# A hybrid decoder step on one core: the sample's state step moved out of the scan, and eight more gate blocks computed as Strassen pairs

## The chip, the core and the metric

The kernel runs on one core of a Trainium2 chip. The core has a matrix engine (TensorE, "PE" in the profile; its weight loads are listed apart as "PEld"), a vector engine (VectorE, "DVE"), an engine for activations and copies (ScalarE, "ACT"), a general engine (GpSimd, "POOL") and a queue engine that issues most of the DMAs (SyncE, "SP"); ACT issues some DMAs too, on a queue of its own. The metric is the device time of one execution in microseconds. The kernel before takes 2536.3 us, the median of 3 runs (2535.32 to 2539.43).

## What is computed

One layer of a decoder for a prompt of 1024 tokens and a sample group of 8 sequences with one token each. Both share all weights, so the kernel carries their 1024 + 8 = 1032 columns through every product together. What matters here, cut from the reference:

```python
splits = [int(v) for v in np.cumsum(IN_SIZES)[:-1]]
sc_b, sc_c, sc_x, z, xbc, dt_raw, q, gates = jnp.split(xn @ w_in, splits, axis=-1)
...
xbc_c, ssm_conv_new = causal_depthwise_conv(xbc, ssm_hist, ssm_conv_w)
xbc_c = jax.nn.silu(xbc_c + ssm_conv_b)
xs, bm, cm = jnp.split(xbc_c, [SSM_D_INNER, SSM_D_INNER + SSM_GROUPS * SSM_STATE], axis=-1)
...
y_ssd, ssm_new = ssd_fn(xs, dt, a, bm, cm, ssm_s0)
...
g_a, g_b, g_c = jnp.split(jax.nn.sigmoid(gates), N_BRANCHES, axis=-1)
merged = g_a * y_a + g_b * y_b + g_c * y_c
```

For the prompt, `ssd_fn` is a chunked scan (8 chunks of 128 tokens, 32 heads in 4 groups). For the sample it is one step of the recurrence, on a state of 32 heads x 64 x 128 for each of the 8 sequences:

```python
s = s * jnp.exp(dtt * a)[..., None, None] + (dtt[..., None] * xt)[..., None] * bh[:, :, None, :]
return s, jnp.einsum('bhpn,bhn->bhp', s, ch)
```

All products are float32, split into a high and a low part, so that each product of weights and activations is three matmuls (high x high, high x low, low x high).

## The kernel before

Everything is laid out with features on the 128 partitions and the 1032 columns in the free dimension. `w_in` is worked through in blocks of 128 output features. There are two ways to compute blocks.

- **Plain block** (`gemm`, line 180): 8 slices of the contraction x 3 split products x 3 column parts of 344 = 72 matmuls.
- **Strassen pair** (`strassen`, line 279): two blocks at once, as seven products of 4 x 3 x 2 = 24 matmuls of 258 columns, 168 in all. It also needs sums of weights (`V.tensor_add` in lines 305 and 306, `st_adds2`), splits of these sums (`st_split`: the high part on ACT, line 224, the low part on DVE, line 225), copies of the products out of PSUM (ACT, lines 296, 315, 318) and combinations of them (DVE, lines 320, 331, 333). The seven products run through three PSUM tiles; some of them are overwritten while the pair is still under way, so that PE can go on only when a copy or a combination has read them.

Work that is to run beside the matmuls is cut into pieces (functions in the deque `pend`). `tick()` takes one piece. A plain block calls it `pace[0]` times, spread over its 8 contraction slices; a pair calls it three times (lines 311, 327, 334). The pieces set an order of priority: a list scheduler orders each engine's instructions at build time, by this order and by its own estimates of when operands are ready. Each engine is given its list in that order.

The order of work around the change:

1. Six pairs of z blocks, with the memory keys and values as pieces (lines 1206 to 1208).
2. The pair stage (lines 1213 to 1230). First the xbc pair (17, 21), then for each of four groups: an xbc pair, three pairs for the short convolution (`sc_pairs`, two "C" pairs and a "B" pair), another xbc pair and one gate pair (`gate_pair`, line 764). After that a z pair, and the xbc pairs (18, 22) and (19, 23); in the last one the activations' second half is restored (`plain`, line 1226). An xbc pair also runs the depthwise convolution of both blocks on DVE (`xbc_conv`, line 707).
3. The scan (lines 1236 to 1306). Four groups of pieces run beside plain blocks: 8 q blocks, 16 gate blocks (8 to 23), then the 8 blocks of the first output projection (`out_part`). A group has 40 pieces: loading its activations, the scan's 8 chunks in three pieces each (`first`, `second`, `third`), then the gating with z and the group norm. With `pace[0] = 5` the 160 pieces take 32 plain blocks.
4. Attention and the remaining 16 projection blocks, then the last projection, the merge, and the feed-forward part.

The sample's state step lies in the scan's pieces: `s_load` (line 927: the state of one sequence and group, 256 KB, and the broadcast B and C rows, 128 KB, both by SP), `s_step` (line 934: 4 activations that decay the state, 4 that form the update, one addition of 512 columns on DVE) and `s_read` (line 943: the store of the new state, 256 KB, a product of 512 columns and a reduction on DVE). There are 32 such steps, 8 in each group. `bc_rows` (line 777) prepares the B and C rows of a group: two PE transposes, a copy and a store. Some of these pieces are held back behind named instructions with `tc.issue_after`.

Of the kernel before, what the change touches and what calls it, by code (L numbers as in the profile page):

```python
# [41 lines left out]
def tile_kernel(ctx: ExitStack, tc, a, o):  # L42
# [135 lines left out]
    pace = [3]  # L178

    def gemm(w, acts, name, width=P, off=0):  # L180

        hi, lo = w
        ps = mm_ps(name)
        nk = len(acts)
        marks = {nk * i // pace[0] for i in range(pace[0])}
        for k, (ah, al) in enumerate(acts):
            if k in marks:
                tick()
            ks = slice(k * width + off, k * width + off + P)
            for i, (wt, x) in enumerate(((hi, ah), (hi, al), (lo, ah))):  # L190
                for n in range(NCH):
                    PE.matmul(  # L192
                        ps[:, n, :CW], wt[:, ks], x[:, n * CW : (n + 1) * CW],
                        start=(k == 0 and i == 0), stop=(k == nk - 1 and i == 2),
                    )
        return ps
# [332 lines left out]
    dpar = cn.tile([P, 16], F32, tag="dpar", name="dpar")  # L529

# [212 lines left out]
    def plain_pair(col, dst, i, nm, func, hook=None):  # L743
# [7 lines left out]
        pa = strassen(  # L751
            wblock(w_in, col + i * P), wblock(w_in, col + (i + 1) * P), xforms, f"{nm}{i}", pa_["s"], outs,
            hook=hook,
        )
# [9 lines left out]
    def gate_pair(i):  # L764
        plain_pair(C_G, gt_d, i, "G", AF.Sigmoid)
# [11 lines left out]
    def bc_rows(g, bcg):  # L777

        ps = sm_ps(f"psbc{g}")
        PE.transpose(ps[:NS, :P], bcg[0][:, T:TT], ident)  # L780
        PE.transpose(ps[:NS, P : 2 * P], bcg[1][:, T:TT], ident)
        t = ev_tile(f"bcr{g}", (NS, 2, P))
        S.copy(t, b3(ps[:NS, : 2 * P], 2))
        SY.dma_start(bc_d[g], t)

    def ssd_pieces(g, xg, bcg):
# [8 lines left out]
        def load(c):  # L795
            nm = f"{g}_{c}"
            r = sp_tile([P, HPG, P], "r", "r" + nm, 3)
            live[c] = r
            return SY.dma_start(r, ac_d[g, c].unsqueeze(0).to_broadcast([P, HPG, P])).ins
# [16 lines left out]
        def first(c):  # L816
# [16 lines left out]
            state["xdt"] = V.tensor_tensor(  # L833
                b3(xdt, HPG), b3(xp, HPG), bc(dtT[:, c, hs].unsqueeze(2), [P, HPG, 64]), op=ALU.mult
            ).ins
# [50 lines left out]
        def decay(c):  # L886

            s_new = sp_tile([P, 512], "s", f"s{g}_{c}")
            ins = G.tensor_tensor(  # L889
                b3(s_new, HPG), b3(state["s"], HPG), bc(cdec[:, c, hs].unsqueeze(2), [P, HPG, 64]),  # L890
                op=ALU.mult,
            )
            state["next"] = s_new
            return ins.ins
# [11 lines left out]
        def s_skip():  # L906
            for t in range(4):
                V.scalar_tensor_tensor(
                    xg[t][:, T:TT], xg[t][:, T:TT], dpar[:, g * 4 + t : g * 4 + t + 1], hold["ys"][:, t, :],
                    op0=ALU.mult, op1=ALU.add,  # L910
                )

        hold = {}

        def s_prep():
            xd = sp_tile([P, 4, NS], "xds", f"xds{g}", 1)
            for t in range(4):
                V.tensor_mul(xd[:, t, :], xg[t][:, T:TT], dts[:, g * 4 + t, :])
            hold["xd"] = xd
            hold["ys"] = sp_tile([P, 4, NS], "ys", f"ys{g}", 1)  # L920

        def s_rows(t, b):
            return t[0, b, hs].rearrange("h p n -> (h p) n").rearrange("(t q) n -> q t n", q=P)

        samp = {}

        def s_load(b):
            st = sp_tile([P, 4, P], "st", f"st{g}_{b}", 3)
            SY.dma_start(st, s_rows(a["state_ssm"], b))
            bcb = sp_tile([P, 2, P], "bcb", f"bcb{g}_{b}")  # L930
            SY.dma_start(bcb, bc_d[g, b].unsqueeze(0).to_broadcast([P, 2, P]))
            samp[b] = (st, bcb)

        def s_step(b):
            st, bcb = samp[b]
            for t in range(4):
                S.activation(st[:, t], st[:, t], AF.Copy, scale=es[:, g * 4 + t, b : b + 1])  # L937
            xb = sp_tile([P, 4, P], "xb", f"xb{g}_{b}", 1)
            for t in range(4):
                S.activation(xb[:, t], bcb[:, 0], AF.Copy, scale=hold["xd"][:, t, b : b + 1])  # L940
            V.tensor_add(st, st, xb)  # L941

        def s_read(b):
            st, bcb = samp.pop(b)
            SY.dma_start(s_rows(o["s_ssm"], b), st)
            xb = ev_tile(f"xc{g}_{b}", (P, 4, P))
            V.tensor_tensor(xb, bc(bcb[:, 1:2, :], [P, 4, P]), st, op=ALU.mult)
            V.tensor_reduce(hold["ys"][:, :, b : b + 1], xb, axis=AX.X, op=ALU.add)

        def head():  # L950
            load(0)
            load(1)
            s_prep()
            prep(0)
            s_load(0)
            s_load(1)
# [3 lines left out]
        for c in range(NCK + 1):  # L960
            def p1(c=c):
                if c < NCK:
                    first(c)
                if c + 2 < NCK:
                    state["load"] = load(c + 2)
                if c > 1:
                    with tc.issue_after(state["xdt"] if c < NCK else state["sum"]):
                        with tc.issue_after(state["load"]):
                            s_read(c - 2)

            def p2(c=c):
                if c > 0:
                    state["sum"] = third(c - 1)
                    with tc.issue_after(state["sum"]):
                        if c < NCK:
                            with tc.issue_after(decay(c)):
                                s_step(c - 1)
                        else:
                            s_step(c - 1)
                if c + 1 < NCK:  # L980
                    with tc.issue_after(state["bT"]):
                        prep(c + 1)
                    if c + 1 > 1:
                        s_load(c + 1)

            def p3(c=c):
                if c < NCK:
                    second(c)
                else:
                    final()  # L990
                    s_read(NCK - 1)
# [232 lines left out]
    xbc_pair(18, 22)  # L1224
# [5 lines left out]
    xbc_pair(19, 23, plain)  # L1230
# [9 lines left out]
    for i in range(8, 24):  # L1240
# [41 lines left out]
    for g in range(GROUPS):  # L1282
# [13 lines left out]
        pend.extend([load_group, None, lambda g=g, bcg=bcg: bc_rows(g, bcg)])  # L1296
# [4 lines left out]
    pace[0] = 5  # L1301
# [562 lines left out]
```

## Time and profile before

| | |
|---|---|
| median of 3 runs | 2536.3 us |
| profiled execution | 2535.69 us |
| its span, first to last instruction | 2533.2 us |
| mean granted TensorE clock | 0.994 |
| PE busy | 2475.3 us (98%) |
| DVE busy | 1502.6 us (59%) |
| ACT busy | 1070.8 us (42%) |
| DMA, mean over the span | 156 GB/s |

A page of the profile describes one execution. It gives the busy time of each engine, the chain of waits that ended last (followed back from the last instruction, each step to what released it), the costliest groups of instructions by source line, and the DMA queues. The trace behind it answers for a window of time, a line or a tile. A row of the windows view lists, after the two ends of the window, its length and then for PE, PEld, DVE, ACT and POOL the busy time with the number of instructions in brackets, then the granted clock, the share of the DMA engines that is busy and GB/s. A row of the chain has its start, its length, the engine and tile, the line, and the number of instructions merged. Ends of matmuls are modelled, and a few per cent of the matmul records are missing, so lengths in the chain are the safer measure for PE.

### The profile page before, as it was taken

The numbers are of one execution on the slowest core, as the hardware profiler recorded it, in microseconds if no ns is written. First come the engines' busy times: TensorE is split into PE (matmuls) and PEld (weight loads), VectorE is DVE, ScalarE is ACT, GpSimd is POOL, SyncE is SP. The second block draws the span as 40 slices with busy tenths as digits, with TensorE's granted clock in tenths as the row PEclk, the third lists the DMA queues.
The fourth block names the chain that finished last, engine by engine and source line by source line (L and its number), as shares of the span: only waits on it lengthen the run. The fifth ranks groups of instructions, "written<-read, shape, count | busy, mean of one in ns | idle before, by whom it ended". The sixth has DMA issues, their size and how long they took to land.

```text
span 2533.2 us, 44306 instructions
## 1 busy us (share of the span) xinstructions
PE 2475.3 (98%) x18505; PEld 2408.9 (95%) x18505; DVE 1502.6 (59%) x2262; ACT 1070.8 (42%) x1783; POOL 115.1 (5%) x139
## 2 busy tenths in 40 slices
PE   7999999999999999999999989999999999999998
PEld 5999999999999999999989888999999999999998
DVE  6754575666666675757687662444776444463326
ACT  6544434343524665867554341223443333341202
POOL 0100000000000121212020000000000000000000
PEclk9999999999999999999999999999999999999999
DMA  6344422322323777676778977944442222274211
GB/s 203 101 155 151 126 84 85 92 87 83 99 76 126 226 226 232 202 240 213 263 232 288 313 254 239 303 144 151 145 135 92 84 68 86 74 240 136 75 34 68
DMA packets 351590, 394.68 MB, mean 156 GB/s; under 512 B 15814, under 2 KB 289302, under 8 KB 351383
## 3 DMA queue, kind: packets, MB, share of 16 engines
q1 hardware_dynamic: 332238, 338.90, 42.9%
q10 hardware_dynamic: 19153, 52.96, 5.5%
q8 instruction: 145, 2.38, 0.4%
q14 instruction: 54, 0.44, 0.1%
HBM read 283.57 MB, written 108.45 MB: 155 GB/s over the span
## 4 chain that ended last, share of the span: by engine, by line
PE 86%; DVE 6%; DMA 5%; ACT 2%; issue 1%; SPq 0%; DVEq 0%; ACTq 0%
PE po L192 12%; PE pd L192 8%; PE ps_g L192 6%; PE pm L1622 4%; PE ps_q L192 4%; PE py L858 1%; PE pss L876 1%; PE po L850 1%; PE ps_z L192 1%; PE X17m L237 1%; PE G2m L237 1%; PE B6m L237 1%; PE X12m L237 1%; PE C5m L237 1%; PE X6m L237 1%
## 5 line engine op out<-in xcount | busy, mean ns | idle before, releaser
L1764 DVE TENSOR_TENSOR x<-pd,x 128x1032 f32<-128x1032 f32 x24 | 29.5, 1230 | 127.2 <-PE pd L192 127.2
L805 ACT ACTIVATE r<-r,acum 128x128 f32<-128x128 f32 x256 | 78.6, 391 | 5.3 <-DMA r<-ac_d 4.8
L1263 DVE TENSOR_TENSOR gt<-po,gt 128x1032 f32<-128x1032 f32 x24 | 29.5, 1230 | 56.5 <-PE po L192 56.5
L837 POOL TENSOR_TENSOR xdd<-xdt,decst 128x512 f32<-128x512 f32 x32 | 48.6, 1518 | 311.3 <-DVE xdt L833 311.3
L940 ACT ACTIVATE xb<-bcb,xds 128x128 f32<-128x128 f32 x128 | 41.9, 391 | 45.7 <-DMA bcb<-bc_d 44.2
L644 DVE SCALAR_TENSOR_TENSOR ax<-u,prm,ax 128x1024 f32<-128x1024 f32 x44 | 56.3, 1280 | 0.2 <-ACT ax L641 0.2
L937 ACT ACTIVATE st<-st,es 128x128 f32<-128x128 f32 x128 | 42.4, 391 | 19.0 <-DMA st<-in_state_ssm_dram 11.3
L831 DVE TENSOR_TENSOR r<-r,cbm 128x1024 f32<-128x1024 f32 x32 | 39.1, 1221 | 12.5 <-ACT r L806 11.2
L867 DVE SCALAR_TENSOR_TENSOR x<-x,dpar,yt 128x128 f32<-128x128 f32 x128 | 36.4, 347 | 14.4 <-ACT yt L865 13.6
L858 PE MATMUL py<-r,xdt 128*64 128x128 f32 x512 | 35.0, 279 | 1.5 <-issue 1.5
L889 POOL TENSOR_TENSOR s<-s,cdec 128x512 f32<-128x512 f32 x28 | 35.4, 1265 | 20.9 <-DVE s L882 20.2
L876 PE MATMUL pss<-xdd,bT 128*128 128x512 f32 x64 | 33.3, 601 | 2.0 <-ACT bT L830 1.8
L806 ACT ACTIVATE r<-r 128x1024 f32<-128x1024 f32 x32 | 33.8, 1056 | 0.3
L1551 DVE TENSOR_TENSOR gt<-po,gt 128x1032 f32<-128x1032 f32 x8 | 9.9, 1232 | 39.3 <-PE po L192 39.3
L858 PEld LDWEIGHTS py<-r,xdt 128*64 128x64 f32 x512 | 27.3, 136 | 5.8 <-issue 2.4
L854 DVE TENSOR_TENSOR yt<-po,ea 128x512 f32<-128x512 f32 x28 | 19.3, 688 | 22.2 <-PE po L850 22.2
L1629 DVE TENSOR_TENSOR x<-pm,xT 128x516 f32<-128x516 f32 x16 | 11.1, 695 | 35.7 <-PE pm L1622 35.6
L850 PE MATMUL po<-bc,s 128*128 128x128 f32 x224 | 29.9, 276 | 2.1 <-DVE s L882 2.1
L850 PEld LDWEIGHTS po<-bc,s 128*128 128x128 f32 x224 | 28.2, 191 | 3.3 <-DVE s L882 3.0
L1372 DVE SCALAR_TENSOR_TENSOR kc<-kc,qb 128x256 f32<-128x256 f32 x64 | 23.8, 418 | 12.3 <-DMA qb<-qs_d 8.6
L941 DVE TENSOR_TENSOR st<-st,xb 128x512 f32<-128x512 f32 x32 | 29.6, 926 | 0.0
L1384 ACT ACTIVATE pr<-psa,mx 128x256 f32<-128x256 f32 x32 | 14.8, 471 | 32.0 <-DVE mx L1382 31.2
(8793 smaller groups left out, 8815.8 us busy)
## 6 DMA issues: line engine op xcount, KB each, us to landing
gt<-gt_d SPq DMA_DIRECT2D x32, 516.0 KB
r<-ac_d SPq DMA_DIRECT2D x32, 512.0 KB
mg_d<-gt SPq DMA_DIRECT2D x24, 516.0 KB
mg<-mg_d SPq DMA_DIRECT2D x24, 516.0 KB
xs_d<-ax ACTq DMA_DIRECT2D x22, 516.0 KB
hr<-h_d SPq DMA_DIRECT2D x22, 516.0 KB
x<-xs_d SPq DMA_DIRECT2D x16, 516.0 KB
zs<-zs_d SPq DMA_DIRECT2D x16, 516.0 KB
```

The costliest lines, as they stand in the source:

```text
L192: PE.matmul(ps[:, n, :CW], wt[:, ks], x[:, n * CW : (n + 1) * CW], start=(k == 0 and i == 0), stop=(k == nk - 1 and i == 2),)
L237: PE.matmul(ps[:, n, :HC], wt[:, ks], x[:, n * HC : (n + 1) * HC], start=(start and kt == 0 and i == 0), stop=(kt == 3 and i == 2), skip_g ...
L644: V.scalar_tensor_tensor(acc[:, :T], u[:, j : j + T], w[j], acc[:, :T], op0=ALU.mult, op1=ALU.add)
L805: S.activation(r[:, j, :], r[:, j, :], AF.Relu, scale=-1.0, bias=acum[:, c, h : h + 1])
L831: V.tensor_tensor(r, r, bc(cbm.unsqueeze(1), [P, HPG, P]), op=ALU.mult)
L837: G.tensor_tensor(b3(xdd, HPG), b3(xdt, HPG), bc(decst[:, c, hs].unsqueeze(2), [P, HPG, 64]), op=ALU.mult)
L850: PE.matmul(po[:, t * P : (t + 1) * P], state["s"][:, t * P : (t + 1) * P], bcg[1][:, cs], start=True, stop=True,)
L858: PE.matmul(py[hp : hp + 64, (h // 2) * P : (h // 2 + 1) * P], xdt[:, h * 64 : (h + 1) * 64], r[:, (h % 2) * 4 + h // 2, :], start=True, s ...
L876: PE.matmul(pss, bT, xdd, start=True, stop=True)
L937: S.activation(st[:, t], st[:, t], AF.Copy, scale=es[:, g * 4 + t, b : b + 1])
L940: S.activation(xb[:, t], bcb[:, 0], AF.Copy, scale=hold["xd"][:, t, b : b + 1])
L1622: PE.matmul(ps[:, n, :HC], wt[:, ks], x[:, half * HT + n * HC : half * HT + (n + 1) * HC], start=(k == 0 and i == 0), stop=(k == KD - 1 an ...
```

## The change

- The sample's 32 state steps leave the scan's pieces. After both xbc pairs of a group, 13 pieces (`s_pieces`) are put in `pend`, to run beside the group's three short-convolution pairs and its gate pairs.
- A step is written differently: 4 activations decay the state (as before); 4 `scalar_tensor_tensor` on DVE of 128 columns form and add the update, and 4 more multiply by C and sum in one instruction (with an accumulator). State and B and C rows now share one activation tile, in one buffer of each of the two tags, so two steps at most are in flight.
- The factor dt x of the sample is formed by POOL in `xbc_conv`, and the sample's B and C columns are collected there. One `bc_rows` with one transpose serves all four groups; its tile is stored once.
- Gate blocks 0 to 15 are pairs (eight `gate_pair`, before four); 16 to 23 stay plain. The plain blocks beside the scan are now 8 q, 8 gates and 8 of the first projection.
- The xbc pairs (18, 22) and (19, 23) come first in the pair stage, and each group's two xbc pairs follow each other. The stage now ends with a z pair and a gate pair, which restores the activations.
- A group of the scan has 39 pieces, and `pace[0]` is 6.5, so 156 pieces take 24 plain blocks.

```diff
-    pace = [3]
+    pace = [3, 0.0]
...
-        marks = {nk * i // pace[0] for i in range(pace[0])}
+        n = int(pace[0] + pace[1])
+        pace[1] += pace[0] - n
+        marks = {nk * i // n for i in range(n)}
...
         S.activation(acc[:, :TT], acc[:, :TT], AF.Silu)
+        if ct < 16:
+            G.tensor_tensor(dts[:, ct, :], acc[:, T:TT], dts[:, ct, :], op=ALU.mult)
+        else:
+            G.tensor_copy(bcs[:, ct % 4, :, ct // 20], acc[:, T:TT])
         S.dma_start(xs_d[ct], acc[:, :TT])
...
+    def bc_rows():
+
+        ps = sm_ps("psbc")
+        PE.transpose(ps[: 8 * NS, :P], bcs.rearrange("p g b w -> p (g b w)"), ident)
+        t = ev_tile("bcr", (8 * NS, P))
+        S.copy(t, ps[: 8 * NS, :P])
+        SY.dma_start(bc_d.rearrange("g b w p -> (g b w) p"), t)
...
+    def s_load(g, b):
+        t = act_tile(("ah", "al")[b % 2], f"st{g}_{b}", F32)
+        SY.dma_start(b3(t[:, :512], 4), s_rows(a["state_ssm"], g, b))
+        SY.dma_start(b3(t[:, 512:768], 2), bc_d[g, b].unsqueeze(0).to_broadcast([P, 2, P]))
+        samp[g, b] = t
+
+    def s_step(g, b):
+        t = samp[g, b]
+        st, junk = b3(t[:, :512], 4), t[:, 768:896]
+        for i in range(4):
+            S.activation(st[:, i], st[:, i], AF.Copy, scale=es[:, g * 4 + i, b : b + 1])
+        for i in range(4):
+            V.scalar_tensor_tensor(
+                st[:, i], t[:, 512:640], dts[:, g * 4 + i, b : b + 1], st[:, i], op0=ALU.mult, op1=ALU.add
+            )
+        for i in range(4):
+            V.scalar_tensor_tensor(
+                junk, st[:, i], 1.0, t[:, 640:768], op0=ALU.mult, op1=ALU.mult,
+                accum_out=ys[:, g * 4 + i, b : b + 1],
+            )
+
+    def s_store(g, b):
+        SY.dma_start(s_rows(o["s_ssm"], g, b), b3(samp.pop((g, b))[:, :512], 4))
+
+    def s_pieces(g):
+
+        out = [lambda: s_load(g, 0)]
+        for b in range(0, NS, 2):
+            out.append(lambda b=b: (s_step(g, b), s_load(g, b + 1)))
+            out.append(lambda b=b: (s_store(g, b), s_step(g, b + 1)))
+            out.append(lambda b=b: (s_store(g, b + 1), s_load(g, b + 2) if b + 2 < NS else None))
+        return out
...
-    xbc_pair(17, 21)
+    for i in (17, 18, 19):
+        xbc_pair(i, i + 4)
+    bc_rows()
     for i in range(4):
         xbc_pair(4 * i, 4 * i + 1)
+        xbc_pair(4 * i + 2, 4 * i + 3)
+        pend.extend(s_pieces(i))
         sc_pairs(2 * i)
-        xbc_pair(4 * i + 2, 4 * i + 3)
-        gate_pair(2 * i)
-    z_pair(14)
+        gate_pair(4 * i)
+        if i < 3:
+            gate_pair(4 * i + 2)
+    flush()
...
-    xbc_pair(18, 22)
+    z_pair(14)
...
-    xbc_pair(19, 23, plain)
+    gate_pair(14, plain)
...
-    for i in range(8, 24):
+    for i in range(16, 24):
         fillers.extend(gate_step(i))
...
-        pend.extend([load_group, None, lambda g=g, bcg=bcg: bc_rows(g, bcg)])
+        pend.extend([load_group, None])
...
-    pace[0] = 5
+    pace[0] = 6.5
```

More of the change, by code (lines that the diff above doesn't have):

```diff
@@ L529, in tile_kernel @@
     dpar = cn.tile([P, 16], F32, tag="dpar", name="dpar")
+    ys = cn.tile([P, 16, NS], F32, tag="ys", name="ys")
+    bcs = cn.tile([P, GROUPS, NS, 2], F32, tag="bcs", name="bcs")
     dt_stack = ExitStack()
@@ L741, in z_step, with plain_pair @@
         S.dma_start(zs_d[i], t[:, :TT])
-    def plain_pair(col, dst, i, nm, func, hook=None):
+    def plain_pair(col, dst, i, nm, func, hook=None, after_t3=None):
         os = []
@@ L752, in plain_pair @@
             wblock(w_in, col + i * P), wblock(w_in, col + (i + 1) * P), xforms, f"{nm}{i}", pa_["s"], outs,
-            hook=hook,
+            hook=hook, after_t3=after_t3,
         )
@@ L762, in z_pair, with gate_pair @@
         plain_pair(C_Z, zs_d, i, "Z", AF.Silu, hook)
-    def gate_pair(i):
-        plain_pair(C_G, gt_d, i, "G", AF.Sigmoid)
+    def gate_pair(i, after_t3=None):
+        plain_pair(C_G, gt_d, i, "G", AF.Sigmoid, None, after_t3)
     ssd = ExitStack()
@@ L775, in sp_tile, with s_rows @@
         return pool["ssd"].tile(shape, F32, tag=tag, bufs=bufs, name=name)
[L777 to L784, printed above, removed]
+    def bc_rows():
[4 more added lines that the diff above has]
+        SY.dma_start(bc_d.rearrange("g b w p -> (g b w) p"), t)
+    def s_rows(t, g, b):
+        h = t[0, b, g * HPG : (g + 1) * HPG]
+        return h.rearrange("h p n -> (h p) n").rearrange("(t q) n -> q t n", q=P)
+    samp = {}
+    def s_load(g, b):
[26 more added lines that the diff above has]
+        return out
     def ssd_pieces(g, xg, bcg):
@@ L798, in load @@
             live[c] = r
-            return SY.dma_start(r, ac_d[g, c].unsqueeze(0).to_broadcast([P, HPG, P])).ins
+            SY.dma_start(r, ac_d[g, c].unsqueeze(0).to_broadcast([P, HPG, P]))
         def prep(c):
@@ L832, in first @@
             xdt = sp_tile([P, 512], "xdt", "xdt" + nm)
-            state["xdt"] = V.tensor_tensor(
+            V.tensor_tensor(
                 b3(xdt, HPG), b3(xp, HPG), bc(dtT[:, c, hs].unsqueeze(2), [P, HPG, 64]), op=ALU.mult
-            ).ins
+            )
             xdd = sp_tile([P, 512], "xdd", "xdd" + nm)
@@ L893, in decay @@
             state["next"] = s_new
-            return ins.ins
         def final():
@@ L908, in s_skip @@
                 V.scalar_tensor_tensor(
-                    xg[t][:, T:TT], xg[t][:, T:TT], dpar[:, g * 4 + t : g * 4 + t + 1], hold["ys"][:, t, :],
+                    xg[t][:, T:TT], xg[t][:, T:TT], dpar[:, g * 4 + t : g * 4 + t + 1], ys[:, g * 4 + t, :],
                     op0=ALU.mult, op1=ALU.add,
                 )
[L913 to L948, printed above, removed]
         def head():
@@ L964, in p1 @@
                 if c + 2 < NCK:
[L965 to L969, printed above, removed]
+                    load(c + 2)
             def p2(c=c):
                 if c > 0:
[L973 to L979, printed above, removed]
+                    ins = third(c - 1)
+                    if c < NCK:
+                        with tc.issue_after(ins):
+                            decay(c)
                 if c + 1 < NCK:
```

8 lines of the change are left out of this document (1 added, 7 removed).

## Prediction

> **What bounds the kernel now.** I read the page's totals first, then the windows view, then the chain of waits, then who waited for whom.
>
> ```profile
> span 2533.2 us, 44306 instructions
> PE 2475.3 (98%) x18505; PEld 2408.9 (95%) x18505; DVE 1502.6 (59%) x2262; ACT 1070.8 (42%) x1783; POOL 115.1 (5%) x139
> PE 86%; DVE 6%; DMA 5%; ACT 2%; issue 1%; SPq 0%; DVEq 0%; ACTq 0%
> ```
>
> PE works for 98% of the span and carries 86% of the chain. As that is an average over stages, the two stages that the change touches have to be read for themselves: a group of the pair stage (404 to 525) and the scan (from 827).
>
> ```profile
> core 0: us, PE busy (x) PEld busy (x) DVE busy (x) ACT busy (x) POOL busy (x), PEclk, DMA share, GB/s
> 404.00:525.00 121.00, 121.00 (x1007) 121.00 (x1006) 79.27 (x106) 49.38 (x59) 3.67 (x12) 1.00 0.29 88
> 827.00:900.00 73.00, 69.50 (x515) 66.25 (x514) 51.55 (x83) 52.19 (x116) 11.73 (x14) 1.00 0.76 235
> 1000.00:1100.00 100.00, 99.20 (x688) 93.03 (x687) 74.11 (x118) 71.78 (x150) 16.26 (x12) 1.00 0.74 227
> 1100.00:1200.00 100.00, 98.86 (x697) 91.55 (x696) 64.33 (x109) 75.50 (x167) 20.72 (x15) 1.00 0.69 210
> 1200.00:1300.00 100.00, 95.59 (x653) 88.93 (x652) 75.34 (x110) 61.72 (x132) 15.14 (x11) 0.98 0.80 264
> ```
>
> In the pair stage PE is never idle, at full clock, with DVE at 66%, ACT at 41% and the DMA engines at 29%. In the scan PE is idle for 3.5, 0.8, 1.1 and 4.4 us in these windows, with the DMA engines at 70 to 80%. Both stages are bound by PE: what the change saves there in matmuls is gained, unless another engine becomes late. PE's waits say where it is late already (first row: the only wait over 0.2 us between 277 and 820; the others: from the end of the pair stage into the scan).
>
> ```profile
> PEld Z14m L237 <- DVE Z14Sl L225: 0.3, 1, 0.3
> PE X19m L237 <- DVE u L331: 1.1, 1, 1.1
> PE ps_q L192 <- ACT u L734: 0.9, 1, 0.9
> PE py L858 <- issue: 1.5, 1, 1.5
> PE po L192 <- ACT b02h L162: 2.0, 1, 2.0
> ```
>
> **The change, part by part.**
>
> *Eight gate blocks as four pairs.* The chain has a pair, and the long run of plain blocks at the end:
>
> ```profile
> 520.49 20.24 PE G2m L237 x168
> 2281.07 199.13 PE pd L192 x1260
> 977.34 0.11 PE psbc L780
> 977.45 0.11 PE psbc L781
> ```
>
> A pair takes 20.24 us. A plain matmul takes 199.13 / 1260 = 0.158 us, a plain block of 72 so 11.38, two 22.76. Each pair saves 2.52 us, four save **10.1 us**. The bounds are narrow: the other gate pairs run in the same stage without a wait.
>
> *bc_rows.* Eight transposes of 0.11 us become one: **-0.8 us**. Its store and broadcast now lie long before their use.
>
> *The state step beside the pairs.* Its cost by rows (a tile's rows have the least, median and greatest ns of one; the page's have the busy us and the mean ns of one):
>
> ```profile
> L937 ACT ACTIVATE st<-st,es 128x128 f32<-128x128 f32 x128 | 42.4, 391 | 19.0 <-DMA st<-in_state_ssm_dram 11.3
> L940 ACT ACTIVATE xb<-bcb,xds 128x128 f32<-128x128 f32 x128 | 41.9, 391 | 45.7 <-DMA bcb<-bc_d 44.2
> L941 DVE TENSOR_TENSOR st<-st,xb 128x512 f32<-128x512 f32 x32 | 29.6, 926 | 0.0
> L947 DVE TENSOR_TENSOR xc<-bcb,st x32: 672/682/1534, 879.7 to 1327.6; 128x512 f32<-128x512 f32 x32
> L948 DVE TENSOR_REDUCE ys<-xc x32: 672/680/690, 881.0 to 1328.3; 128x4 f32<-128x512 f32 x32
> L867 DVE SCALAR_TENSOR_TENSOR x<-x,dpar,yt 128x128 f32<-128x128 f32 x128 | 36.4, 347 | 14.4 <-ACT yt L865 13.6
> L1372 DVE DVE_READ_ACCUMULATOR kc<-kc,qb x64: 78/81/86, 1386.0 to 1482.8; 128x1 f32 x64
> ```
>
> Before, a step has 8 activations of 391 ns (3.1 us of ACT) and 926 + 682 + 680 ns = 2.3 us of DVE. After, it has 4 activations (1.6 us) and 8 operations of 128 columns, 8 x 347 ns, with four accumulator reads of 81 ns: 3.1 us of DVE. A group's eight steps put 25 us of DVE and 12.5 us of ACT beside the pairs. A group also gets one more gate pair; I price it at the group's mean, 79.27 / 6 = 13.2 us of DVE and 49.38 / 6 = 8.2 of ACT, which is too much, since a gate pair has no convolution. DVE then works (79.3 + 13.2 + 25) / (7 x 20.24) = 83% of the time, ACT (49.4 + 8.2 + 12.5) / 141.7 = 49%. Neither becomes the bound by its total.
>
> What counts is lateness at single points. Seven products share three PSUM tiles, and a product takes 20.24 / 7 = 2.89 us. Where a tile is written again one product later, the read of it has 2.89 us. On DVE such a read is:
>
> ```profile
> 555.20 0.69 DVE L331 TENSOR_TENSOR u<-u,X8m 128x516 f32<-128x516 f32 x1 [0.81 <-PE X8m L237]
> ACT xb L940 <- DMA bcb<-bc_d: 44.2, 21, 6.8
> SPq L218 <- DVE C2sb L271: 16.8, 1, 16.8
> ```
>
> So there are 2.2 us to spare. A burst of 3.1 us of step work ahead of the read overruns that by 0.9 at most, 32 x 0.9 = 29 us if every step hit it. A step must start in 0.9 us of a pair's 20.24 to do so, which happens to one or two steps: 1 us.
>
> The other danger is a late load. The step waits on ACT for the state, on DVE for the B and C rows, and behind either stand the copies and combinations that PE waits for. The second row of the fence shows such waits in the scan: 21 in 32 steps, mean 2.1, longest 6.8 us. At the mean PE loses nothing (2.1 is under 2.2); if all 32 were the longest it would lose 32 x 4.6 = 147 us. These are the ends. I am near the lower one, because the DMA engines are 29% busy in the pair stage against the scan's 74%: a loss in a few steps, 2 us. Together **+3 us**, with the ends 0 and 147. Nothing here can be a gain, since PE has no idle time in that stage.
>
> [...]
>
> SP gets 96 more DMAs in the pair stage. A store waits for the step, a load for the store two steps earlier, and the weight loads queue behind them. The third row shows that cover: SP itself waits 16.8 of a pair's 20.24 us for a weight buffer, and that pair's matmuls still did not wait. Price 0; without this cover, a pair late by the length of a store. POOL gets 24 small operations, and is busy 3.67 us in 121: 0.
>
> *The end of the pair stage.* X19 had its own convolution backlog from X18 and the restoring of the activations, and PE waited 1.1 + 0.9 us around it. Now a gate pair behind a z pair ends the stage, with no convolution. I take **-1.5 us** (between 0 and the 3.5 us of idle in that window).
>
> *The scan with 24 plain blocks.* These rows mark the ends of three groups (psf), the first scan matmul of the next group (bp), and one chunk:
>
> ```profile
> 946.86 0.44 PE psf L899 x4
> 1072.10 0.44 PE psf L899 x4
> 1107.06 0.11 PE bp L822
> 1197.68 0.44 PE psf L899 x4
> ...
> 883.12 0.89 PE po L850 x8
> 893.94 0.89 PE po L850 x8
> ```
>
> A group takes 125.2 and 125.6 us, of which 8 blocks x 11.38 = 91.0. With 6 blocks it is 125.4 - 22.8 = 102.7 us. Can the others keep up? From the end of a group to the next one's first matmul 35.0 us pass (1072.1 to 1107.1), a chain of gating, norm, stores and loads that the change leaves alone except for bc_rows. That leaves 102.7 - 35.0 = 67.7 us for eight chunks, 8.5 us each; now a chunk takes 10.8. ACT, at 71.78 us in a window of 100, has 90 in a group; less the sample's 84.3 / 4 = 21 it has 69 of 102.7. DVE, at 74.11, has 93; less 8 x 2.3 = 18 it has 75. The change from gate blocks to projection blocks moves from between two groups into the last chunk of the third one; PE waited 2.0 us there for the split of an input (b02h), and I keep that. The scan's queue on SP loses the sample's 96 DMAs. So the scan can follow, and what PE waited for in it can shrink: **-1 us** (between -4 and, below, a loss).
>
> *The sum*, against the profiled execution's own 2535.69 us (span 2533.2 and 2.5 around it): -10.1 - 0.8 + 3 - 1.5 - 1 = -10.4, so 2525.3. That execution is 0.6 us under the median of 2536.3, so the median should come to **2526 us** (-0.41%).
>
> **The rivals.**
>
> 1. *Late steps hold up the pairs (slower).* On ACT or DVE a step is placed where the scheduler expects its load; the two buffers make each load wait for the store two steps back, so a late landing hands its delay on. The forecast without the 3 us is 13.4 us ahead; this rival decides when the 32 steps lose over 13.4 / 32 = 0.42 us each, waits of 2.6 us. At waits of 3.2 us a step loses 1.0, 32 us in all: 2536 - 13.4 + 32 = 2555. For it speak the 21 waits in the scan; against it, the DMA share of 0.29, and that the pair stage's weight loads never stopped PE.
> 2. *The scan is bound by itself (slower).* If a chunk cannot come under 9.5 us, a group takes 35.0 + 76 = 111, 8.3 more than PE needs, 33 in four: 2526 + 33 = 2559. It decides over 10.4 / 4 = 2.6 us a group. Against it: neither ACT nor DVE comes to 75% by the totals above. For it: PE must run plain blocks ahead for 35 us at each change of group, while 12 pieces at 6.5 a block set 21 us there.
> 3. *A small loss in each step (no change).* A third of a us lost in each step and no gain in the scan: 2536.3 - 13.4 + 10.7 + 1 = 2535, within 0.2%.
>
> **How the numbers follow.** The forecast holds with 0.62, rival 1 with 0.16, rival 2 with 0.08, rival 3 with 0.14. The forecast's own range is 2519 (all of the idle time gained, no loss) to 2531. Rivals 1 and 2 are cut where 2 in 10 remain outside, most of it above: 2519 to 2549. About 0.2% (5 us) is what a measurement can tell from no change; faster by more: 0.62, within it: 0.14, slower: 0.24.
>
> **What would show it.** Right: gate pairs of 20.2 us without PE waits between 277 and some 930; groups of the scan 103 us apart; eight fewer plain gate blocks. Wrong: waits of PE for copies or combinations in pairs that have steps beside them, behind ACT waiting for the state or DVE for the B and C rows (rival 1); waits of PE for the scan's state, or groups 110 us apart (rival 2). The prediction falls if DVE's order puts steps ahead of combinations more often than a random place would.

## Result and the profile after

The change makes the kernel slightly slower: 2543.95 us (median of 20 runs, 2537.62 to 2546.92) against 2539.09 us of the kernel before on the same chip (20 runs, 2529.12 to 2545.52). The ratio is 1.002, with a 95% interval of 1.0012 to 1.0029. The forecast was 2526 us. The profiled execution took 2541.26 us, 5.6 more than that of before. The totals and the chain of the page after:

```profile
span 2539.5 us, 44748 instructions
PE 2468.5 (97%) x18594; PEld 2400.7 (95%) x18594; DVE 1512.5 (60%) x2570; ACT 1029.7 (41%) x1664; POOL 130.0 (5%) x163
PE 79%; DVE 9%; DMA 7%; ACT 2%; issue 2%; SPq 0%; POOL 0%; ACTq 0%; DVEq 0%
```

PE is busy for 6.8 us less, and yet the span is 6.3 us longer. The chain has moved: PE carries 79% of it instead of 86%, DVE 9% instead of 6%, DMA 7% instead of 5%.

The starts of first matmuls cut the span into stages: the pair stage runs from tile X17m to the first q block, the scan from there to the first block of the second projection, attention from there to the third block of the fourth projection.

| us | before | after | difference | without loss |
|---|---|---|---|---|
| up to the pair stage | 277.3 | 279.5 | +2.2 | 0 |
| pair stage (28, then 32 pairs) | 570.0 | 666.1 | +96.1 | +80.9 (4 x 20.23) |
| scan (32, then 24 plain blocks) | 508.6 | 414.5 | -94.1 | -91.0 (8 x 11.38) |
| attention | 291.5 | 293.5 | +2.0 | 0 |

So the scan gains a little more than its eight blocks, and the pair stage gives back 15.2 us. The loss has a place. From first matmul to first matmul nearly every pair takes 20.23 us; long are the second C pair and the B pair of each group, with 22.4 and 22.5 in the first group, 22.1 and 22.5, 22.2 and 21.9, 21.9 and 22.4 in the others: 16.0 us over eight pairs' 161.8. Another 1.5 go at the first group's two xbc pairs, ahead of which `bc_rows` now stands (PE waits there 0.2 us for the transpose's input, which POOL collects behind the convolution of the pairs before, and 0.6 us for a split of weights on DVE; the rest is not listed as a wait, and all versions of the new order lose it), and the end of the stage gives 2.4 back: 15.1. The 2.2 and 2.0 us of the two other stages stay open: over all runs of this document the first one lies between 277.3 and 280.4 us, and attention, in the versions with 24 plain blocks, between 290.8 and 295.6. Windows of the first group: C1 and B0 for all engines, and then C0, C1, B0 and the first gate pair for the sample's tiles on DVE alone:

```profile
core 0: us, PE busy (x) PEld busy (x) DVE busy (x) ACT busy (x) POOL busy (x), PEclk, DMA share, GB/s
402.60:425.10 22.50, 20.80 (x170) 20.41 (x170) 20.40 (x68) 9.15 (x20) 1.23 (x2) 1.00 0.62 171
425.10:447.60 22.50, 20.79 (x171) 20.37 (x170) 18.41 (x37) 11.00 (x22) 1.13 (x1) 1.00 0.48 131
```

```profile
core 0: us, DVE busy (x), PEclk, DMA share, GB/s
382.40:402.60 20.20, 3.58 (x19) 1.00 0.52 162
402.60:425.10 22.50, 9.11 (x51) 1.00 0.62 171
425.10:447.60 22.50, 3.11 (x16) 1.00 0.48 131
447.60:467.80 20.20, 0.00 (x0) 1.00 0.33 105
```

The pieces put two steps in each of C0, C1, B0 and the gate pair. In fact the steps run ahead of their pieces: half of the group's work on DVE lies in C1 alone and none in the gate pair; the first eight decays on ACT, those of two states, run at 132 to 140 us already, among the z pairs. PE is idle for 1.7 us in each of the two long windows; the other half us of each is not listed as a wait. Who waits (PE's waits of the pair stage and the first of the scan, then ACT's):

```profile
PE C1m L240 <- ACT c L299: 1.7, 1, 1.7
...
PE B0m L240 <- ACT b L299: 1.4, 1, 1.4
...
PE py L906 <- issue: 4.9, 1, 4.9
...
ACT st L811 <- DMA st<-in_state_ssm_dram: 43.7, 17, 5.6
ACT sacc L643 <- DVE su L671: 25.2, 8, 4.4
```

PE waits for ACT's copy of the first product (line 299 after the change, 296 before). ACT has not been busy; it has itself waited, 17 times, 43.7 us in all, for the sample's state. ACT's copy of the first product in the C1 pair and ACT's own order around the start of the B0 pair, at 425.1, and then the hole that the late copy of C1 leaves on PE (start, length, instruction, idle time before it):

```profile
409.92 0.57 ACT L299 COPY c<-C1m 128x516 f32<-128x516 f32 x1
...
422.95 1.28 ACT L811 ACTIVATE st<-st,es 128x128 f32<-128x128 f32 x4 [4.86 <-DMA st<-in_state_ssm_dram]
425.14 0.69 ACT L811 ACTIVATE st<-st,es 128x128 f32<-128x128 f32 x2 [0.91 <-DMA st<-in_state_ssm_dram]
...
429.82 1.16 ACT L643 ACTIVATE sacc<-su,prm 128x1024 f32<-128x1024 f32 x1 [2.45 <-DVE su L671]
...
431.46 1.03 ACT L227 CAST B0Th<-B0sb 128x1024 fp32r<-128x1024 f32 x1
432.39 0.58 ACT L299 COPY b<-B0m 128x516 f32<-128x516 f32 x1
```

```profile
408.44 0.40 PE L240 MATMUL C1m<-T12ah,C1Sl 128*128 128x258 f32 x2
410.54 0.51 PE L240 MATMUL C1m<-nT20ah,C1Sh 128*128 128x258 f32 x2 [1.70 <-ACT c L299]
```

The first product of B0 was ready near 428.0 (425.1 and 2.89), its copy came at 432.4: the state landed late (ACT idle 4.86 us), the step's DVE work came late with it, the last operation of the C pair's gating (`su`, line 671) stood behind that on DVE, the convolution's first activation (line 643) waited for `su`, and the copy stood behind all of it on ACT. The chain of waits of this window shows where the lateness starts:

```profile
418.51 3.59 DMA out_s_ssm_dram<-st
422.24 2.79 DMA st<-in_state_ssm_dram
425.14 0.07 ACT st L811
...
428.86 0.26 DVE st L813
429.12 0.62 DVE su L671
429.82 0.85 ACT sacc L643
...
432.49 0.49 ACT b L299
433.03 0.99 PE B0m L240 x6
```

From the store of a step to the first decay of the next state in that buffer 6.6 us pass (418.51 to 425.14: a store of 3.59, a load of 2.79). A step that is put as early as its buffer allows therefore stands on ACT and waits for a transfer: 17 times for a state here, and 4 times for the B and C rows (3.7 us). The step itself cost what the rows of before said:

```profile
L811 ACT ACTIVATE st<-st,es 128x128 f32<-128x128 f32 x128 | 42.3, 395 | 50.7 <-DMA st<-in_state_ssm_dram 43.7
L813 DVE SCALAR_TENSOR_TENSOR st<-st,dts 128x128 f32<-128x128 f32 x128 | 41.6, 348 | 18.8 <-ACT st L811 9.4
L817 DVE SCALAR_TENSOR_TENSOR st<-st 128x128 f32<-128x128 f32 x128 | 36.7, 287 | 0.8
```

### The profile page after: what moved, and what is told of

Read it like the earlier page. It is cut to its first block, busy times and chain, and to the rows that moved or that the text cites. A ratio compares the mean times of both kernels' runs of the same rounds, so it can differ in the third digit from the quotient of the medians.

```text
span 2539.5 us, 44748 instructions
## 1 busy us (share of the span) xinstructions
PE 2468.5 (97%) x18594; PEld 2400.7 (95%) x18594; DVE 1512.5 (60%) x2570; ACT 1029.7 (41%) x1664; POOL 130.0 (5%) x163
## 4 chain that ended last, share of the span: by engine, by line
PE 79%; DVE 9%; DMA 7%; ACT 2%; issue 2%; SPq 0%; POOL 0%; ACTq 0%; DVEq 0%
PE po L195 11%; PE pd L195 8%; PE pm L1624 4%; PE ps_g L195 3%; PE ps_q L195 3%; PE py L906 1%; PE pss L924 1%; PE po L898 1%; DVE ax L649 1%; PE ps_z L195 1%; DMA st<-bc_d 1%; PE X17m L240 1%; PE u20m L240 1%; PE G14m L240 1%; PE G12m L240 1%
## 5 line engine op out<-in xcount | busy, mean ns | idle before, releaser
L811 ACT ACTIVATE st<-st,es 128x128 f32<-128x128 f32 x128 | 42.3, 395 | 50.7 <-DMA st<-in_state_ssm_dram 43.7
L885 POOL TENSOR_TENSOR xdd<-xdt,decst 128x512 f32<-128x512 f32 x32 | 40.7, 1271 | 316.6 <-DVE xdt L881 316.6
L813 DVE SCALAR_TENSOR_TENSOR st<-st,dts 128x128 f32<-128x128 f32 x128 | 41.6, 348 | 18.8 <-ACT st L811 9.4
L878 ACT COPY bT<-bp 128x128 f32<-128x128 f32 x32 | 8.4, 264 | 88.6 <-DVE cbm L876 88.5
L817 DVE SCALAR_TENSOR_TENSOR st<-st 128x128 f32<-128x128 f32 x128 | 36.7, 287 | 0.8
```

The lines of the kernel that those rows point to most:

```text
L811: S.activation(st[:, i], st[:, i], AF.Copy, scale=es[:, g * 4 + i, b : b + 1])
L813: V.scalar_tensor_tensor(st[:, i], t[:, 512:640], dts[:, g * 4 + i, b : b + 1], st[:, i], op0=ALU.mult, op1=ALU.add)
L885: G.tensor_tensor(b3(xdd, HPG), b3(xdt, HPG), bc(decst[:, c, hs].unsqueeze(2), [P, HPG, 64]), op=ALU.mult)
```

## Experiments

Three theories were put to the first test. A: the steps stand where the build-time order put them, early and bunched, and hold up copies and combinations there. B: the step's work is too much for a pair that also has a convolution, wherever it lies. C: the loss comes from the rest (fuller scan, more pairs, new order). Stage lengths below are read as in the table above; each time stands beside the kernel before on the same chip.

### One part alone: the gates (e1), the step (e2), no step (e3)

The kernel before with eight gate pairs and 24 plain blocks, its step still in the scan:

```diff
-        gate_pair(2 * i)
+        gate_pair(4 * i)
+        gate_pair(4 * i + 2)
...
-    for i in range(8, 24):
+    for i in range(16, 24):
...
-    pace[0] = 5
+    pace[0] = 20 / 3
```

> The kernel before with one part of the change: gate blocks 0 to 15 as eight pairs, 24 plain blocks beside the scan at 6.67 pieces each (160 pieces); the state step stays in the scan, and the order of the xbc pairs stays. If the step beside the pairs is what took the gain (theory A or B), the pair stage is 32 pairs of 20.2 us without waits of PE (650 us with its ends), and the whole is 8 to 11 us under before, less what the fuller scan loses. If the denser scan or the added pairs themselves cost it (theory C), it is no faster than before, with waits of PE in the scan or in gate pairs.

The kernel after with four gate pairs and 16 plain gates (lines joined; the last gate pair computes block 6 instead of 14):

```diff
-        gate_pair(4 * i)
-        if i < 3: gate_pair(4 * i + 2)
+        if i < 3: gate_pair(2 * i)
...
-    for i in range(16, 24):
+    for i in range(8, 24):
...
-    pace[0] = 6.5
+    pace[0] = 4.875
```

> The other part alone: the kernel after with four gate pairs as before, 16 plain gate blocks and 4.875 pieces a block, the state step beside the pairs. Theory A or B: PE waits 1.5 to 2 us in the second C pair and in the B pair of each group as in the kernel after, 4.4 us a group, about 15 to 18 us in all, and the whole is 10 to 18 us over before. Theory C: no more than 3 us over before.

The kernel after without the sample's state step; it leaves the sample's state out altogether:

```diff
+    V.memset(ys, 0.0)
...
-        pend.extend(s_pieces(i))
```

> The kernel after without the sample's state step: nothing of the sample's state is loaded, computed or stored, and the sums over the state are zero; so the sample's output and its new state are not computed. Theory A or B: the waits in the C and B pairs go, the pair stage falls from 666 to about 650 us, the whole by 15 to 18 us against the kernel after. Theory C: the waits in the pairs stay, and it gains under 4 us.

Measured, beside 2534.94 us of the kernel before:

| | us (median) | ratio, 95% interval | pair stage | scan |
|---|---|---|---|---|
| e1, gates alone | 2534.31 | 1.000 (0.999 to 1.001) | 649.9, 32 pairs | 426.3 |
| e2, step alone | 2545.75 | 1.0044 (1.0032 to 1.0057) | 584.0, 28 pairs | 505.7 |
| e3, no step | 2524.56 | 0.9961 (0.9949 to 0.9974) | 653.6, 32 pairs | 414.5 |

Without the step no C or B pair is longer than 20.23 us (e3's last pair takes 24.7 us, against 21.1 after the change, with a wait of 1.8 us for a combination on DVE); with the step alone the pair stage grows by 14 us. So the loss belongs to the step. e1 holds the other half: its pairs are perfect (79.9 us for four more), and yet nothing is gained, since the scan with 24 blocks and the steps in it takes 426.3 us, 8.7 over 508.6 - 91.0. The same scan matmuls (4 of each group, first and last start) in e1, and in the kernel after:

```profile
L901 PE MATMUL psf<-ident,s x16: 270/272/273, 1010.4 to 1334.0; 128*128 128x128 f32 x16
```

```profile
L946 PE MATMUL psf<-ident,s x16: 271/273/273, 1031.9 to 1339.0; 128*128 128x128 f32 x16
```

Three groups take 323.6 us in e1, 107.9 each, against 307.1 and 102.4 after: where the step stays in the scan, the scan is bound by itself. PE then waits for group norm and copies (`psnr` 3.2 us, `pss` 2.9 us):

```profile
PE psnr L1046 <- DVE nr L1038: 3.2, 1, 3.2
PE pss L878 <- ACT bT L832: 2.9, 4, 1.2
```

### The same step, held in its place (e4)

```diff
+            held["act"] = S.copy(h3(o12), hv(pa)).ins        # the pair's last copy on ACT
+            held["dve"] = V.tensor_tensor(...o11...).ins     # and, at two places, its
+        held["dve"] = V.tensor_tensor(...o12...).ins         # latest combination on DVE
...
+    def s_pinned(g, b):
+        with tc.issue_after(held["act"]), tc.issue_after(held["dve"]):
+            s_step(g, b)
```

> The kernel after with the same work, but each step held behind two instructions of the pair in which its piece is taken: its activations behind the copy of the third product, its DVE operations behind a combination. So two steps lie in each of four pairs, instead of some running far ahead of their place. Theory A (steps placed by the scheduler where their load is late, bunched in two pairs): most of the 4.4 us a group goes, pair stage 650 to 655 us, the whole 10 to 15 us under the kernel after. Theory B (too much DVE work in pairs that have a convolution, wherever it lies): the waits stay or grow, pair stage 660 us or more.

2522.84 us, ratio 0.9954 (0.9941 to 0.9967); pair stage 650.1 us, scan 415.2. It is 0.7% under the kernel after by the two ratios, with the same instructions. The sample's DVE work by pair (C0, C1, B0, gate; columns as above), and the chain from 400 to 434 us, which was one of DMA, ACT and DVE after the change:

```profile
380.70:400.90 20.20, 3.77 (x19) 1.00 0.45 138
400.90:421.20 20.30, 4.49 (x26) 1.00 0.43 118
421.20:441.40 20.20, 4.15 (x24) 1.00 0.52 143
441.40:461.60 20.20, 4.44 (x24) 1.00 0.57 170
```

```profile
399.89 1.20 PE C0m L241 x10
401.09 20.23 PE C1m L241 x168
421.32 12.76 PE B0m L241 x106
```

Two steps lie in each pair, ACT never waits for the state, and PE works through. DVE does the same work in pairs that have a convolution, and the DMA engines are about as busy (0.43 to 0.57) as in the kernel after (0.48 to 0.62 in the pairs with steps). A holds; B falls, and the DMA share by itself is not the cause. C explains e1, not the loss after the change.

### Late loads or bunched work (e5, e6, e8)

Holding the steps takes away two things at once: waits for loads on ACT (A1) and bunched work on DVE (A2). The hold on ACT alone (e5), the hold on DVE alone (e6), and no hold, but with the loads and stores of six of each group's eight states left out (e8):

```diff
-        with tc.issue_after(held["act"]), tc.issue_after(held["dve"]):
+        with tc.issue_after(held["act"]):      # e5; in e6: held["dve"]
```

```diff
     def s_load(g, b):
+        if b > 1:
+            samp[g, b] = samp[g, b % 2]
+            return
...
-        SY.dma_start(s_rows(o["s_ssm"], g, b), b3(samp.pop((g, b))[:, :512], 4))
+        t = samp[g, b]
+        if b > 5:
+            SY.dma_start(s_rows(o["s_ssm"], g, b), b3(t[:, :512], 4))
```

> As the pinned version (2522.8 us), but the steps are held behind the pair's copy on ACT alone (L323), not behind its combinations on DVE. The hold on ACT decides when a step's four decays run, and the step's work on DVE needs the decays. Two theories on what in the early, bunched steps of the changed kernel held PE up. A1, late loads on ACT: the decays wait there for a state that is still on its way, and the copies behind them are late. Then this hold alone gives nearly the whole gain: 2522 to 2527 us, the second C pair and the B pair of a group take under 20.7 us each. A2, bunched work on DVE: the steps' operations of 128 columns stand ahead of the splits and combinations. Then this run is also good as far as the hold on ACT spreads them, but should lose 0.3 us or more in each pair that has steps, 2528 to 2535. Neither: 2540 or more, if a hold on one engine does not keep the steps where they are.

> The counterpart: steps held behind the combinations on DVE alone (L320, L333). The decays on ACT may then be put ahead as far as the two buffers let them. A1 (late loads on ACT): the waits of ACT for the state stay, and most of the loss: 2533 to 2544 us, waits of PE for copies of the products C1m and B0m as before. A2 (bunched work on DVE): 2522 to 2527. But since a buffer comes free only when the step's work on DVE is done and its store has landed, this hold also delays the loads, so that the decays cannot run far ahead: if it gives the whole gain as the hold on ACT does, the two are not told apart by these two runs, and the run without the reloads decides.

> The changed kernel, steps not held, but in each group the state and the B and C rows are loaded for the first two sequences only, and the other six steps work on these two tiles again; stored are only the last two. So three quarters of the sample's state are neither loaded nor stored, and its time is that of the same work on ACT and DVE without the waits for loads. A1 (late loads on ACT): the waits of ACT for the state are gone and PE's waits in the second C pair and the B pair with them; 32 pairs in 650 to 654 us, 2522 to 2528 us. A2 (bunched work on DVE): the steps are bunched as much or more, since no load holds them back; 2535 us or more, waits in the first C pair instead of the later ones. 2528 to 2535: both have a share.

Measured, beside 2534.77 us: e5 2525.97 us (0.9965, 0.9954 to 0.9976), e6 2524.63 (0.9963, 0.9950 to 0.9975), e8 2524.47 (0.9963, 0.9951 to 0.9974); pair stages 650.2, 651.2 and 651.9 us. Either hold is enough, so e5 and e6 do not tell the two apart; for e6, A1 had asked for 2533 us or more, with this outcome named as the one that decides nothing. e8 does tell them apart. The sample's DVE work of its first group in C0 and C1 (columns as above):

```profile
383.30:403.50 20.20, 4.86 (x30) 1.00 0.33 106
403.50:423.70 20.20, 8.71 (x50) 1.00 0.33 89
```

C1 has 50 such instructions, as bunched as the 51 after the change, and takes 20.23 us; of all C and B pairs only B2 is longer, by 0.9. PE's wait there and ACT's waits in e8, and ACT's waits in e6:

```profile
PE B2m L240 <- ACT b L299: 0.6, 1, 0.6
...
ACT st L814 <- DVE st L820: 39.4, 22, 3.4
ACT st L814 <- DMA st<-in_state_ssm_dram: 9.9, 3, 4.3
```

```profile
ACT st L812 <- DMA st<-in_state_ssm_dram: 21.0, 20, 2.8
```

Even the 0.9 us stand behind a late load: B2 follows the longest of e8's three waits for a state, 4.3 us (that load could start only when the bunched work had freed its buffer), and behind the other two, 2.6 and 2.9 us, nothing is lost. In the kernel after, each of the eight long pairs follows one wait of 3.3 to 5.6 us for a state. So bunched work alone costs next to nothing, and it is not the sum of the waits either: 39.4 us of ACT's waits for DVE in e8 cost nothing that can be put down to them, 21.0 us of waits for the state, none over 2.8, nothing but 0.7 us in the C2 pair of e6; 43.7 us with single ones up to 5.6 cost 16 after the change. One reserve: without the loads the build-time order of e8 is another one, so the two differ in more than the transfers.

### The scan's start (e7)

```diff
+    pa_["u"] = ev_tile
     gate_pair(14, plain)
```

> The pinned version with one line more: the last gate pair puts its sums in the tiles of another pool, so that the scan's first loads need not wait until the stores of that pair have landed. In the changed kernel and in the pinned version PE waits 4.9 us for the scan's first product (py). If that wait is one for memory, it falls to 1.5 us or less, and the time by 3 to 5 us: 2518 to 2520. If the loads are late for another reason (the DMA queue, or the activations' second half), the wait stays and the time is 2522 to 2524.

2517.32 us, ratio 0.9932 (0.9918 to 0.9947): the best version, 0.2% under e4 by the two ratios, whose intervals just overlap, and a little more than was foreseen. PE's wait for `py`, 5.0 us in the pinned version, is 0.8 for another operand, and the scan takes 406.5 us instead of 415.2. A wait of DVE in the kernel after, at the scan's start, and PE's wait in e7:

```profile
DVE cbm L876 <- DMA gt_d<-G: 6.3, 1, 6.3
```

```profile
PE py L911 <- DMA ea<-ea_d: 0.8, 1, 0.8
```

The first scan operation on DVE waits for the store of a gate block that it has nothing to do with but memory: the scan's tiles lie where the last gate pair's sums lay.

### The step moved and held, without more gate pairs (e9)

Edit: the pins of e4 in the kernel of e2.

> The state step moved beside the pairs and pinned there, with the four gate pairs of before and 16 plain gate blocks (pace 4.875). Theory A: the pin takes away the 14 us that the pair stage lost in the run with the step alone (2545.8), so 2530 to 2533 us, 28 pairs in 569 to 572 us; and the scan stays at 505 us, since with 32 plain blocks beside it PE was the bound there with the step too. The move alone is then worth 3 to 5 us, the four pairs alone nothing (2534.3 before), and both together 11: they need each other. If the step's work cost the pairs anything even where it is pinned, 2536 or more.

2529.94 us beside 2535.25, ratio 0.9984 (0.9976 to 0.9993); 28 pairs in 569.4 us, scan 506.8. The step's move alone is worth 0.16%, the gates alone nothing (e1), both 0.46% (e4): with 32 blocks beside it the scan hid the step almost for nothing, with 24 it cannot.

### How late a copy may be (e10, e11)

In the C and B pairs of the pinned version the first product is copied again:

```diff
             S.copy(h3(o11), hv(pa))
+            for _ in range(4 if nm[0] in "CB" else 0):    # e11: 8
+                S.copy(h3(o11), hv(pa))
```

> The pinned version, and in the twelve C and B pairs the copy of the first product out of PSUM is done four times more (the same values to the same place), before ACT goes on. This delays the release of that PSUM tile by about 4 x 0.5 = 2 us. The next product but one is written to it, one product of 2.89 us after the first; with 0.5 us for the copy itself some 2.2 us should be to spare. So PE should wait for next to nothing, 0 to 0.4 us a pair: 2522 to 2528 us. If there is less to spare than the prediction took, PE waits 0.5 us or more in each of the twelve pairs.

> As with four copies more, but eight: some 4 us late, 1.6 to 2 us over what is to spare. PE should wait that long in each of the twelve C and B pairs, as it does in the changed kernel (1.4 to 1.7 us in the second C pair and the B pair): pairs of 21.8 to 22.3 us, the pair stage 19 to 24 us longer, 2541 to 2548 us. If ACT catches up elsewhere, or another read of that tile had set the release, the loss is smaller than 1 us a pair.

2530.57 and 2540.02 us, pair stages 656.5 and 666.0: 0.53 and 1.3 us for each of the twelve pairs. Four copies cost more than foreseen, eight less. The measure is not a clean one, because the build-time order knows of these copies and moves PE's work around them: PE takes up the first product of the next pair before the last one of this pair (chain of e11, where two pairs alternate):

```profile
443.82 1.08 PE G0m L241 x9
444.90 2.89 PE B0m L241 x24
447.79 2.19 PE G0m L241 x18
```

So these two runs do not measure what is to spare. The trace after the change does, in two pairs: the copies of C1 and B0 start at 409.92 and 432.39, 4.4 us behind the end of the first product (402.67 and 425.10, each with 2.89), and the pairs lose 2.2 and 2.3 us. Some 2.1 us were to spare, against the prediction's 2.2.

### Two gate pairs more (e12)

On the version of e7, gate blocks 16 to 19 as pairs, 20 plain blocks beside the scan, pace 7.8.

> The version pinned and with the scan's memory freed early (2517.3 us), with gate blocks 16 to 19 as two pairs more (34 pairs) and 20 plain blocks beside the scan (pace 7.8). It asks where the scan becomes the bound by itself. If PE is still the bound in the scan with 20 blocks: the pairs take 40.5 us more, the scan 45.5 less (361 us), 2512 us. If a group cannot come under some 100 us (the scan's chain of gating, norm and loads, 35 us, and eight chunks), the scan takes 380 us or more and the time is 2530 or more. Between them: a mean of 1 to 4 us lost in each group, 2514 to 2528.

2525.16 us, ratio 0.9964 (0.9951 to 0.9978): 7.8 us over e7. The pairs cost 40.4 us, the scan gains 39.9 (366.6) where 45.5 were to be had, and attention loses 7.2, since the last group's output comes late for the projection behind it. PE's waits in e12, in the scan and in attention:

```profile
PE xp L879 <- DMA x<-xs_d: 4.1, 3, 2.1
...
PE po L195 <- ACT b00h L162: 9.5, 1, 9.5
```

A group takes 91.7 us in the mean (366.6 / 4), where 90.3 would be left if PE were the only bound ((406.5 - 45.5) / 4): here the scan begins to wait for its own loads, and what is late at its end is paid for in attention.

## Why the prediction was wrong

- **The gate pairs (-10.1): right; bc_rows (-0.8): not shown by itself.** In e4 four pairs more take 80.1 us and the scan is 93.4 shorter; the sum, -13.3, is what the prediction had ahead of the +3 (-13.4). That the two agree so closely is luck in part: the end of the pair stage with `py` came out 2.6 us worse there, the pairs behind `bc_rows` 1.5 worse, and the scan without `py` 4.1 better. The gain is there only if the scan can follow, and it follows only without the step (e1 against e4). The prediction took the step out of the scan's load in its working, but did not say that the pairs by themselves would bring nothing.
- **The state step beside the pairs (+3): the step that failed.** Measured are 16 us: eight pairs of 1.7 to 2.3 us. Of the two ways named there, the burst on DVE was rightly priced low, as far as e8 shows. The late load was not. Four things in its working were wrong. The row of 21 waits that it read is ACT's wait for the B and C rows; for the state ACT waited 11.3 us before, and it is the state that it waited for after the change, 43.7 us, with 3.7 for the B and C rows. "At the mean PE loses nothing (2.1 is under 2.2)" took a mean where each wait counts by what it has over the slack: the mean is 2.57 after the change (43.7 / 17), but one wait of 3.3 to 5.6 us comes before each of the eight late copies. "I am near the lower one, because the DMA engines are 29% busy" took the share of a stage without the step's own transfers; with them it is 0.48 to 0.62 in the pairs with steps, and e4 shows that even a share of 0.43 to 0.57 need not cost anything. And the pieces were read as places. They are only an order of priority, so a step is put as early as its buffer allows, 6.6 us behind the store of the state that lay there before, and 17 times ACT waited there for a state that was still on its way. No step was at "a random place".
- **Rival 1 was the case.** It decided from 0.42 us a step; 16.0 / 32 = 0.50 were lost. In the trace after, the late copies stand on ACT behind work that waited: the one at 432.39 follows decays that waited 4.86 us for the state and an activation that waited 2.45 us for `su`, though the product it reads was ready near 428.0. The waits in the scan of before (44.2 us of ACT for the B and C rows, where no entry of PE's waits is over 2.1 us) had little to say about a stage with some 2.1 us to spare.
- **The end of the pair stage (-1.5): wrong in sign.** The last xbc and z pairs lost 2.4 us less, but PE's wait for `py` grew from 1.5 to 4.9, as the scan's memory came free only with the last gate pair's store. Net +1.0; e7 takes it away.
- **The scan (-1 beside its blocks and bc_rows): right in sign, too small.** -94.1 stands against -91.0 - 0.8 - 1 = -92.8, but the 3.4 us more of `py` lie in it; without them it is -97.5. Groups are 102.4 us apart, 102.7 forecast. The rest has a place and no shown reason: the ends of the third and the fourth group, which the prediction did not read, are 131.3 us apart before and 101.0 after. Rival 2 did not come, but its mechanism is real: it takes the gain in e1 and begins to bind in e12.
- **SP and POOL (0): right** as far as PE's waits show; none in the pair stage is for a weight load, and one of 0.2 us is for POOL.
- **The sum:** with the step held, the forecast's -0.41% stands beside -0.46% measured (e4).

## What to carry to other kernels

Work that begins with a transfer and is put on an engine ahead of urgent work is to be priced neither by its busy time nor by a mean wait, but by its longest waits against the slack of what stands behind it (here 3.3 to 5.6 us against some 2.1). Try to hold it behind the last urgent instruction of the stretch: in e4 ACT's waits for the state in the pair stage fell from 43.7 us to 0, the stage from 666.1 to 650.1 us, with the scan at 415.2 against 414.5, a gain of 0.7%. When work is thinned beside a chain that it covers (here 32 to 24 blocks), ask first whether the chain is short enough, and move what makes it long in the same change: each alone gave 0 and 0.16%, both 0.46%.

## What the runs showed that was not expected

- At the change from the pair stage to the scan, tiles of a new pool waited for the store of the tile that lay there before: 6.3 us on DVE by the trace, and by e7 most of PE's 4.9 (listed as "issue"; 0.8 for another operand in e7). Another place for one pair's sums was worth some 5.5 us (e4 to e7).
- ACT stood idle for DVE 39.4 us in 22 waits without a loss on PE that follows from them (e8), while 43.7 us in 17 waits for loads cost 16: the sum of an engine's waits said little here.
- A delay that was known at build time was partly arranged away in e11: eight copies more cost 1.3 us a pair, where 8 x 0.5 us less the 2.2 to spare would be 1.8.
